# Moving a recurrence's copies to ScalarE, its output to a PSUM bank of its own, weight low parts to VectorE, and masks to fills

## The chip, the core and the metric

One core of one Trainium2 chip runs the whole program once. The metric is device time in microseconds (us) of one execution. The engines of the core are TensorE (PE in the profile; its weight loads are PEld), VectorE (DVE), ScalarE (ACT), GpSimd (POOL) and SyncE (SP). Each works through its own queue of instructions in order and waits on semaphores of the others.

## The reference

The program is a stack of layers on 512 tokens of width 1024: two layers of a first block (neighbourhood attention, differential attention, convolution), and then a second block of two layers, each with a feed-forward part, a mixer and another feed-forward part. Only the two mixers of the second block are touched here. The first mixer is a delta-rule recurrence over tokens, beside a gated linear recurrence:

```python
def rwkv7_step(S, inp):
    r_t, w_t, k_t, v_t, kk_t, a_t = inp
    sa = jnp.einsum("bhvk,bhk->bhv", S, -kk_t)
    S = (S * w_t[:, :, None, :]
         + jnp.einsum("bhv,bhk->bhvk", sa, kk_t * a_t)
         + jnp.einsum("bhv,bhk->bhvk", v_t, k_t))
    y = jnp.einsum("bhvk,bhk->bhv", S, r_t)
    return S, y
```

The second mixer is a stick-breaking attention, whose mask is strict (a token does not see itself):

```python
mask = k_pos[None, :] < q_pos[:, None]
log_1m = jnp.where(mask, jax.nn.log_sigmoid(-z), 0.0)
between = lax.cumsum(log_1m, axis=3, reverse=True) - log_1m
att = jnp.where(mask, jnp.exp(jax.nn.log_sigmoid(z) + between), 0.0)
```

## The kernel before

Everything is kept on the core. Large products are made in a split form: a weight chunk of 128x1024 is loaded by SyncE's DMA queue, ScalarE rounds it to its high part `whi` (line 366), another engine subtracts to get the low part `wlo` (line 368), and TensorE multiplies hi by hi, lo by hi and hi by lo (line 574). Which engine makes the low part is decided by name in `wchunk`: GpSimd for the chunks of the two mixers (`ein`, `eo`, `sq`, `sk`, `sv`), apart from five listed in `BEGIN`, and VectorE for all others. Of the 22 chunks of the first mixer's input projection (`ein`), 19 have their low part made by GpSimd.

**First mixer (`even`).** Eight heads are handled as four pairs, and the 512 tokens as eight chunks of 64. For each pair, `prep`, `inverse` and `tokens` work out the chunk matrices (mostly small VectorE operations), and `recur` then walks the eight chunks in order. The next pair's preparation and the projections' products are woven between the steps of `recur`, and a priority scheduler fixes the order of each engine when the program is built. A chunk of `recur` takes one PSUM bank `pc` (the profile calls it `mm`; the tag has two buffers) and goes: two products of the state `VS` with `G` (line 1747), a copy of the first to `Xs` by VectorE (1749) and of the second to `ya` by ScalarE (1750), a product with `Y` (1753), two copies of its halves into `VS`, one by ScalarE and one by VectorE (1755), a product with `B` that gives the next state (1759) and one with `MTr` that gives the rest of the output (1761), then the next state as the product plus the decayed state `SD` by VectorE (1767), `SD` for the chunk after by GpSimd (1771), and `ya` plus the second part by VectorE (1772). All five products of a chunk lie in columns of the one bank.

**Second mixer (`stick`).** For each of eight head pairs and four query blocks (32 units, of 512, 384, 256 and 128 keys), TensorE makes the scores (1406), ScalarE makes two sigmoids, `o` and `b` (1410, 1411), GpSimd masks the last 128 columns: `o` by a multiplication and an addition, `b` by a multiplication (1413 to 1415), with two 128x128 tables in `bc`; VectorE then runs a reversed running product over `o` for each of the two heads (1421), multiplies it into `b` (1422), and TensorE transposes `b` (1431) and multiplies by the values (1449). The projections of the next pair (line 574) run between.

Of the kernel before, what the change touches and what calls it, by code (L numbers as in the profile page):

```python
# [11 lines left out]
F32 = mybir.dt.float32  # L12
# [74 lines left out]
BEGIN = [('ein', 12), ('ein', 13), ('ein', 8), ('sv', 0), ('sk', 0)]  # L87
# [200 lines left out]
class Kern:  # L288
# [63 lines left out]
    def wchunk(self, name, i, n, split=True, extra=False, slot=None):  # L352
# [14 lines left out]
        eng = nc.gpsimd if name in ('ein', 'eo', 'sq', 'sk', 'sv') and (name, i) not in BEGIN else nc.vector  # L367
# [986 lines left out]
    def stick(self, sp, oh, ol, out):  # L1354
# [5 lines left out]
        bc = sp.tile([128, 2, 128], F32, name="bc")  # L1360
        nc.gpsimd.dma_start(bc, a['before'].rearrange("p (j n) -> p j n", j=2))
        before, notbefore = [bc[:, j].unsqueeze(1).to_broadcast([128, 2, 128]) for j in range(2)]
# [30 lines left out]
        class Unit:  # L1393
# [5 lines left out]
            def S(s):  # L1399
# [11 lines left out]
                nc.scalar.activation(b[:, :, :n], z[:, :, :n], AF.Sigmoid, scale=0.125)  # L1411
                d = slice(n - 128, n)
                nc.gpsimd.tensor_tensor(o[:, :, d], o[:, :, d], before, ALU.mult)  # L1413
                nc.gpsimd.tensor_tensor(o[:, :, d], o[:, :, d], notbefore, ALU.add)  # L1414
                nc.gpsimd.tensor_tensor(b[:, :, d], b[:, :, d], before, ALU.mult)
# [68 lines left out]
    def even(self, sp, oh, ol, room, out):  # L1484
# [251 lines left out]
        def recur(pr):  # L1736
# [5 lines left out]
            for c in range(8):  # L1742
                pc = self.mm()
                for j, cs in ((0, slice(0, 64)), (1, slice(192, 256))):
                    for h in range(2):
                        kr = slice(0, 128) if c else H[1 - h]
                        nc.tensor.matmul(pc[H[h], cs], G[h][kr, c, j], VS[kr, h, c], start=True, stop=True)
                Xs = sp.tile([128, 64], F32, name="Xs", tag="Xs", bufs=2)
                nc.vector.tensor_copy(Xs, pc[:, 0:64])
                nc.scalar.copy(ya[:, c], pc[:, 192:256])  # L1750
# [3 lines left out]
                for h in range(2):  # L1754
                    (nc.vector.tensor_copy if h else nc.scalar.copy)(VS[H[h], h, c], pc[H[h], 64:128])
# [4 lines left out]
                for h in range(2):  # L1760
                    nc.tensor.matmul(pc[H[h], 256:320], MTr[H[h], c], VS[H[h], h, c], start=True, stop=True)
                if c < 7:
                    for h in range(2):
                        if SD is None:
                            (nc.vector.tensor_copy if h else nc.scalar.copy)(VS[H[h], h, c + 1], pc[H[h], 128:192])
                        else:
                            nc.vector.tensor_tensor(VS[H[h], h, c + 1], pc[H[h], 128:192], SD[H[h]], ALU.add)
                if c < 6:
                    SD = sp.tile([128, 64], F32, name="SD", tag="SD", bufs=2)
                    for h in range(2):  # L1770
                        nc.gpsimd.tensor_scalar(SD[H[h]], VS[H[h], h, c + 1], dc[H[h], c + 1:c + 2], None, ALU.mult)
# [314 lines left out]
```

## Time and profile before

| | us |
|---|---|
| median of three runs | 3127.25 (3127.15 to 3130.33) |
| the profiled execution, its own time | 3127.6 |
| its span in the trace | 3125.4 |
| first mixer, from its first projections to the end of its recurrence | 1337 to 1690 |
| of that, the 32 chunks of the recurrence | 1403 to 1677 |
| second mixer, its 32 units | 2475 to 2725 |

The sum in the prediction is made against the profiled execution's 3127.6 us, which is 0.35 us above the median; the span and 2.2 us around it make it up. Positions such as 1403 are microseconds from the span's start. In the rows further down, the idle time of an engine is followed by what ended it ("<-ACT ya L1750" is ScalarE's write of `ya` on line 1750), and a granted clock of 1.00 is 2.4 GHz, one of 0.50 is 1.2 GHz.

### The profile page before, as it was taken

Reading aid. Unit: us, or ns where it says so; the run is one execution under the profiler, and the core shown is the slowest. Engines: PE = TensorE matmul, PEld = TensorE weight load, DVE = VectorE, ACT = ScalarE, POOL = GpSimd, SP = SyncE. Lnnn points to the kernel's source line nnn. Section 1 sums busy time; section 2 is a strip of 40 time slices with the busy share of each in tenths; the row PEclk is TensorE's granted clock in tenths of the full one; section 3 lists DMA queues with packets and bytes.
Section 4 is the critical chain, followed back from the end, with each engine's and each line's share of the span. In section 5 each row is a group of like instructions: output and inputs, shape, how many; then the busy total and the mean of one; then the engine's idle time right before and its main releaser. Section 6 shows DMA issues by size and latency. Waiting matters only on the chain. (4 is left out here: it accounts for less than half of the span.)

```text
span 3125.4 us, 47823 instructions
## 1 busy us (share of the span) xinstructions
PE 2968.1 (95%) x18806; PEld 2544.0 (81%) x18806; DVE 2198.8 (70%) x3818; ACT 1434.9 (46%) x2501; POOL 481.2 (15%) x597
## 2 busy tenths in 40 slices
PE   7999999999999999988898999989999988889998
PEld 4987887798878989865556899979898766779897
DVE  5968674767767949568774976859495566779494
ACT  5358654437644535342323544435353444445352
POOL 3010010111001000143334100010000455310000
PEclk9999999999999999999879999999999999999999
DMA  5232123231232423421003332433334211223233
GB/s 201 95 123 77 40 70 110 72 108 62 63 111 92 125 85 99 152 81 41 21 21 115 97 123 85 141 116 96 94 109 146 66 48 48 77 86 119 88 93 127
DMA packets 81681, 290.69 MB, mean 93 GB/s; under 512 B 9264, under 2 KB 9616, under 8 KB 81328
## 3 DMA queue, kind: packets, MB, share of 16 engines
q1 hardware_dynamic: 68688, 241.35, 24.4%
q10 hardware_dynamic: 7200, 26.22, 2.3%
q0 software_dynamic: 5568, 20.07, 2.0%
q8 instruction: 148, 2.42, 0.3%
q14 instruction: 77, 0.63, 0.1%
HBM read 272.92 MB, written 14.68 MB: 92 GB/s over the span
## 5 line engine op out<-in xcount | busy, mean ns | idle before, releaser
L366 ACT CAST whi<-wraw 128x1024 fp32r<-128x1024 f32 (+2 forms) x300 | 298.3, 1002 | 459.3 <-PE gm L574 120.2
L368 DVE TENSOR_TENSOR wlo<-wraw,whi 128x1024 fp32r<-128x1024 f32 (+2 forms) x254 | 300.2, 1189 | 271.4 <-ACT whi L366 265.0
L605 PE MATMUL acc<-whi,ah 128*128 128x512 f32 x704 | 225.2, 394 | 0.0
L605 PE MATMUL acc<-wlo,ah 128*128 128x512 f32 x704 | 225.0, 394 | 0.0
L605 PE MATMUL acc<-whi,al 128*128 128x512 f32 x704 | 224.7, 393 | 0.0
L574 PE MATMUL gm<-hh,whi 128*128 128x512 f32 (+1 forms) x752 | 210.0, 398 | 3.1 <-DVE ol L416 1.9
L400 ACT CAST whi<-wraw 128x512 fp32r<-128x512 f32 (+1 forms) x152 | 126.9, 837 | 168.3 <-PE acc L701 94.2
L574 PE MATMUL gm<-hl,whi 128*128 128x512 f32 (+1 forms) x752 | 195.6, 393 | 1.1 <-DVE hl L551 1.1
L574 PE MATMUL gm<-hh,wlo 128*128 128x512 f32 (+1 forms) x752 | 193.4, 391 | 0.0
L449 POOL DMA_DIRECT2D gb<-rows x13 | 7.5, 579 | 1193.2 <-DMA x<-xd 563.1
L605 PEld LDWEIGHTS acc<-whi,al 128*128 128x128 f32 x704 | 132.2, 188 | 30.7
L574 PEld LDWEIGHTS gm<-hl,whi 128*128 128x128 f32 x752 | 134.4, 197 | 27.4 <-DVE hl L551 1.8
L605 PEld LDWEIGHTS acc<-wlo,ah 128*128 128x128 f32 x704 | 131.9, 188 | 30.0
L574 PEld LDWEIGHTS gm<-hh,wlo 128*128 128x128 f32 x752 | 132.6, 194 | 28.8 <-issue 3.7
L401 DVE TENSOR_TENSOR wlo<-wraw,whi 128x512 fp32r<-128x512 f32 (+1 forms) x152 | 144.9, 955 | 15.9 <-ACT whi L400 15.8
L605 PEld LDWEIGHTS acc<-whi,ah 128*128 128x128 f32 x704 | 131.6, 188 | 29.6
L574 PEld LDWEIGHTS gm<-hh,whi 128*128 128x128 f32 x752 | 131.4, 195 | 29.3 <-PE gm L1384 2.9
L401 DVE TENSOR_TENSOR wlo<-s,whi 128x1024 fp32r<-128x1024 f32 x76 | 93.0, 1223 | 62.0 <-ACT whi L400 58.6
L368 POOL TENSOR_TENSOR wlo<-wraw,whi 128x1024 fp32r<-128x1024 f32 x46 | 118.2, 2571 | 88.9 <-PE gm L574 31.7
L400 ACT CAST whi<-uraw 128x1024 fp32r<-128x1024 f32 x76 | 79.9, 1051 | 94.5 <-issue 51.8
L1421 DVE TENSOR_TENSOR_SCAN o<-o,zero 128x512 f32<-128x512 f32 (+3 forms) x64 | 84.7, 1360 | 31.7 <-POOL o L1414 31.6
L701 PE MATMUL acc<-hh,wlo 128*128 128x256 f32 x608 | 96.5, 281 | 0.0
(586 smaller groups left out, 7614.9 us busy)
## 6 DMA issues: line engine op xcount, KB each, us to landing
wraw<-l_ffn SPq DMA_DIRECT2D x180, 512.0 KB, 3.7
uraw<-l_ffn SPq DMA_DIRECT2D x76, 512.0 KB, 3.6
wraw<-w_mod SPq DMA_DIRECT2D x48, 512.0 KB, 3.6
x<-xd ACTq DMA_DIRECT2D x24, 512.0 KB, 6.8
wraw<-ein SPq DMA_DIRECT2D x22, 512.0 KB, 3.6
xd<-x ACTq DMA_DIRECT2D x20, 512.0 KB, 2.6
wraw<-w_out SPq DMA_DIRECT2D x16, 512.0 KB, 3.6
gb<-rows POOLq DMA_DIRECT2D x13, 512.0 KB, 8.2
```

The costliest lines, as they stand in the source:

```text
L366: nc.scalar.copy(h[:, :n], r[:, :n])
L368: eng.tensor_tensor(l[:, :n], r[:, :n], h[:, :n].bitcast(F32), ALU.subtract)
L400: nc.scalar.copy(h, src)
L401: nc.vector.tensor_tensor(l, src, h.bitcast(F32), ALU.subtract)
L449: (q or self.nc.gpsimd).dma_start(g, self.a['rows'][ROWS.index(name):ROWS.index(name) + 1, :].broadcast_to([128, D]))
L574: self.nc.tensor.matmul(p, ww[:, k, :], hx[:, k, sl] if tiles is None else part(hx[:, k]), start=(n == 0), stop=(n == 3 * KC - 1))
L605: nc.tensor.matmul(accs[s], ax[:, k, t * 128:(t + 1) * 128], ws[ci][wi][:, (k - c0) * 512:(k - c0 + 1) * 512], start=(ci == 0 and pi == 0 ...
L701: self.nc.tensor.matmul(p, ws[wi][:, k], x[xi][:, k], start=n == 0, stop=n == 11)
L1421: nc.vector.tensor_tensor_scan(ro, ro, zero.to_broadcast([128, n]), 1.0, ALU.mult, ALU.add)
```

## The change

In the first mixer each chunk of the recurrence takes two banks instead of one: the output products go to `py`, where the second is accumulated onto the first by TensorE, so the early copy to `ya` and the late addition become one ScalarE copy at the chunk's end. `Xs`, both halves of `VS` and `SD` are made by ScalarE (the first state, which has no `SD`, is copied by VectorE in both halves). The low parts of all `ein` chunks are made by VectorE. In the second mixer the three masking operations and their table become two `affine_select` on GpSimd, which write a constant where the position is masked.

```diff
-BEGIN = [('ein', 12), ('ein', 13), ('ein', 8), ('sv', 0), ('sk', 0)]
+BEGIN = [('sv', 0), ('sk', 0)]
...
-        eng = nc.gpsimd if name in ('ein', 'eo', 'sq', 'sk', 'sv') and (name, i) not in BEGIN else nc.vector
+        eng = nc.gpsimd if name in ('eo', 'sq', 'sk', 'sv') and (name, i) not in BEGIN else nc.vector
...
-        bc = sp.tile([128, 2, 128], F32, name="bc")
-        nc.gpsimd.dma_start(bc, a['before'].rearrange("p (j n) -> p j n", j=2))
-        before, notbefore = [bc[:, j].unsqueeze(1).to_broadcast([128, 2, 128]) for j in range(2)]
+        one, nought = nc.gpsimd.to_reg(1.0), nc.gpsimd.to_reg(0.0)
...
-                nc.gpsimd.tensor_tensor(o[:, :, d], o[:, :, d], before, ALU.mult)
-                nc.gpsimd.tensor_tensor(o[:, :, d], o[:, :, d], notbefore, ALU.add)
-                nc.gpsimd.tensor_tensor(b[:, :, d], b[:, :, d], before, ALU.mult)
+                for u, fill in ((o, one), (b, nought)):
+                    nc.gpsimd.affine_select(u[:, :, d], u[:, :, d], pattern=[[0, 2], [-1, 128]], base=0, channel_multiplier=1,
+                                            compare_op=ALU.is_gt, fill=fill)
...
-                pc = self.mm()
-                for j, cs in ((0, slice(0, 64)), (1, slice(192, 256))):
+                pc, py = self.mm(), self.mm()
+                for j, p in ((0, pc), (1, py)):
                     for h in range(2):
                         kr = slice(0, 128) if c else H[1 - h]
-                        nc.tensor.matmul(pc[H[h], cs], G[h][kr, c, j], VS[kr, h, c], start=True, stop=True)
+                        nc.tensor.matmul(p[H[h], 0:64], G[h][kr, c, j], VS[kr, h, c], start=True, stop=j == 0)
...
-                nc.vector.tensor_copy(Xs, pc[:, 0:64])
-                nc.scalar.copy(ya[:, c], pc[:, 192:256])
+                nc.scalar.copy(Xs, pc[:, 0:64])
...
-                    (nc.vector.tensor_copy if h else nc.scalar.copy)(VS[H[h], h, c], pc[H[h], 64:128])
+                    nc.scalar.copy(VS[H[h], h, c], pc[H[h], 64:128])
...
-                    nc.tensor.matmul(pc[H[h], 256:320], MTr[H[h], c], VS[H[h], h, c], start=True, stop=True)
+                    nc.tensor.matmul(py[H[h], 0:64], MTr[H[h], c], VS[H[h], h, c], start=False, stop=True)
...
-                            (nc.vector.tensor_copy if h else nc.scalar.copy)(VS[H[h], h, c + 1], pc[H[h], 128:192])
+                            nc.vector.tensor_copy(VS[H[h], h, c + 1], pc[H[h], 128:192])
...
-                        nc.gpsimd.tensor_scalar(SD[H[h]], VS[H[h], h, c + 1], dc[H[h], c + 1:c + 2], None, ALU.mult)
-                nc.vector.tensor_tensor(ya[:, c], ya[:, c], pc[:, 256:320], ALU.add)
+                        nc.scalar.activation(SD[H[h]], VS[H[h], h, c + 1], AF.Copy, scale=dc[H[h], c + 1:c + 2])
+                nc.scalar.copy(ya[:, c], py[:, 0:64])
```

The line numbers of the changed kernel are one lower in this part. On VectorE, in the first pair's recurrence, before (`w`, `G`, `MTa` belong to the next pair's preparation):

```order
L1755 COPY VS<-mm 64x64
L1602 SCALAR_TENSOR_TENSOR w<-k,vecs,acc 128x512
L1767 TENSOR_TENSOR VS<-mm,SD 64x64
L1608 SCALAR_TENSOR_TENSOR G<-w,Dx 64x8x64
L1612 SCALAR_TENSOR_TENSOR w<-w 128x512
L1608 SCALAR_TENSOR_TENSOR G<-w,Dx 64x8x64
L1613 SCALAR_TENSOR_TENSOR w<-w 128x512
L1615 TENSOR_SCALAR w<-w,hv 128x512
L1767 TENSOR_TENSOR VS<-mm,SD 64x64
L1616 SCALAR_TENSOR_TENSOR w<-w,k 128x512
L1772 TENSOR_TENSOR ya<-ya,mm 128x64
L1619 TENSOR_TENSOR w<-w 128x512
```

and at the same place now:

```order
L1601 SCALAR_TENSOR_TENSOR w<-k,vecs,acc 128x512
L1766 TENSOR_TENSOR VS<-mm,SD 64x64
L1607 SCALAR_TENSOR_TENSOR G<-w,Dx 64x8x64
L1611 SCALAR_TENSOR_TENSOR w<-w 128x512
L1607 SCALAR_TENSOR_TENSOR G<-w,Dx 64x8x64
L1612 SCALAR_TENSOR_TENSOR w<-w 128x512
L1614 TENSOR_SCALAR w<-w,hv 128x512
L1766 TENSOR_TENSOR VS<-mm,SD 64x64
L1615 SCALAR_TENSOR_TENSOR w<-w,k 128x512
L368 TENSOR_TENSOR wlo<-wraw,whi 128x1024
L1618 TENSOR_TENSOR w<-w 128x512
```

The copy into `VS` and the addition into `ya` have left the queue, and a low part of a projection chunk stands in it. On ScalarE, in the same recurrence, before (`shl` is a step of the projections):

```order
L366 CAST whi<-wraw 128x1024
L1750 COPY ya<-mm 128x64
L1755 COPY VS<-mm 64x64
L366 CAST whi<-wraw 128x1024
L1541 ACTIVATE shl<-gm,vecs 128x512
L366 CAST whi<-wraw 128x1024
L1750 COPY ya<-mm 128x64
```

and now:

```order
L366 CAST whi<-wraw 128x1024
L1770 ACTIVATE SD<-VS,dc 64x64 x2
L1749 COPY Xs<-mm 128x64
L1754 COPY VS<-mm 64x64 x2
L1770 ACTIVATE SD<-VS,dc 64x64 x2
L1771 COPY ya<-mm 128x64
L366 CAST whi<-wraw 128x1024
```

All steps of a chunk but the new state now stand in one row on ScalarE, between the casts. On GpSimd in the second mixer, one unit and the low part behind it, before:

```order
L1413 TENSOR_TENSOR o<-o,bc 128x2x128
L1415 TENSOR_TENSOR b<-b,bc 128x2x128
L1414 TENSOR_TENSOR o<-o,bc 128x2x128
L368 TENSOR_TENSOR wlo<-wraw,whi 128x1024
L1413 TENSOR_TENSOR o<-o,bc 128x2x128
```

and now:

```order
L1413 AFFINE_SELECT o<-o 128x2x128
L1413 AFFINE_SELECT b<-b 128x2x128
L368 TENSOR_TENSOR wlo<-wraw,whi 128x1024
L1413 AFFINE_SELECT o<-o 128x2x128
L1413 AFFINE_SELECT b<-b 128x2x128
```

One operation fewer stands ahead of VectorE's running product, and the orders of TensorE, VectorE and ScalarE in the second mixer are unchanged.

## Rows read from the trace of the kernel before

**Rows 1.** The page's first part: busy time, share and instructions of each engine.

```profile
PE 2968.1 (95%) x18806; PEld 2544.0 (81%) x18806; DVE 2198.8 (70%) x3818; ACT 1434.9 (46%) x2501; POOL 481.2 (15%) x597
```

**Rows 2.** Busy time in stretches: length, engines, granted clock, DMA share, GB/s.

```profile
1403.00:1677.00 274.00, 245.47 (x1896) 157.65 (x1893) 204.87 (x619) 85.33 (x169) 111.18 (x134) 0.88 0.11 34
...
2475.00:2725.00 250.00, 221.50 (x1192) 174.05 (x1191) 174.03 (x202) 115.23 (x194) 132.95 (x113) 0.95 0.18 53
```

**Rows 3.** Waits of TensorE, 1403 to 1677: us in total, times, longest.

```profile
PE mm L1747 <- DVE VS L1767: 5.7, 5, 2.6
PE mm L1759 <- DVE VS L1755: 4.9, 5, 2.8
...
PE mm L1753 <- ACT ya L1750: 2.6, 4, 0.9
```

**Rows 4.** Waits of VectorE, the same stretch.

```profile
DVE VS L1755 <- ACT VS L1755: 11.1, 10, 3.4
...
DVE Xs L1749 <- PE mm L1747: 6.8, 10, 1.3
```

**Rows 5.** Waits of ScalarE, the same stretch.

```profile
ACT ya L1750 <- DVE Xs L1749: 51.4, 21, 6.2
ACT whi L366 <- PE gm L574: 42.8, 10, 9.6
```

**Rows 6.** Groups by form on VectorE, 1337 to 1690: busy, mean ns, idle before.

```profile
L1755 DVE COPY VS<-mm 64x64 f32<-64x64 f32 x32 | 7.2, 227 | 11.9 <-ACT VS L1755 11.1
...
L1772 DVE TENSOR_TENSOR ya<-ya,mm 128x64 f32<-128x64 f32 x32 | 7.0, 220 | 1.8 <-PE mm L1761 1.0
L1749 DVE COPY Xs<-mm 128x64 f32<-128x64 f32 x32 | 6.9, 219 | 7.0 <-PE mm L1747 6.8
```

**Rows 7.** Groups by form on ScalarE, 1337 to 1690.

```profile
L1755 ACT COPY VS<-mm 64x64 f32<-64x64 f32 x32 | 6.5, 205 | 32.8 <-PE mm L1753 29.8 <-PE acc L1633 3.0
```

**Rows 8.** Groups by form on GpSimd, 1337 to 1690.

```profile
L368 POOL TENSOR_TENSOR wlo<-wraw,whi 128x1024 fp32r<-128x1024 f32 x23 | 57.6, 2504 | 58.8 <-issue 27.6 <-PE gm L574 25.6 <-ACT whi L366 3.9
L1771 POOL TENSOR_SCALAR SD<-VS,dc 64x64 f32<-64x64 f32 x48 | 25.9, 540 | 45.9 <-DVE VS L1767 31.6 <-DVE Z L1706 7.3 <-ACT VS L1765 4.2
```

**Rows 9.** The page's costliest groups: low parts made by VectorE, whole program.

```profile
L368 DVE TENSOR_TENSOR wlo<-wraw,whi 128x1024 fp32r<-128x1024 f32 (+2 forms) x254 | 300.2, 1189 | 271.4 <-ACT whi L366 265.0
```

**Rows 10.** Timeline of VectorE, first mixer: start, us, instruction.

```profile
1421.19 0.16 DVE L436 SCALAR_TENSOR_TENSOR rs_tw<-rs_tw,rs_vw 128x8 f32<-128x8 f32 x1
...
1422.35 2.34 DVE L436 SCALAR_TENSOR_TENSOR rs_tw<-rs_tw,rs_vw 128x8 f32<-128x8 f32 x1
```

**Rows 11.** Timeline of GpSimd, the same place.

```profile
1422.31 2.35 POOL L368 TENSOR_TENSOR wlo<-wraw,whi 128x1024 fp32r<-128x1024 f32 x1
```

**Rows 12.** The chain that ended last, 2525 to 2600: start, us, what.

```profile
2524.40 0.74 POOL o L1413
...
2525.22 0.74 POOL o L1414
...
2525.98 3.94 DVE o L1421 x2
...
2544.25 1.74 POOL o L1413
...
2546.07 0.74 POOL o L1414
...
2546.84 4.45 DVE o L1421 x2
...
2551.93 5.50 PE gm L1449 x24
```

**Rows 13.** Waits of TensorE, 2440 to 2725.

```profile
PE gm L1449 <- DVE ql L416: 14.1, 5, 2.9
```

**Rows 14.** Groups by form on GpSimd, whole program: operations on 256 columns.

```profile
L550 POOL TENSOR_SCALAR hT<-hT,mod 128x256 f32<-128x256 f32 x8 | 9.3, 1164 | 13.7 <-ACT ch L549 13.7
...
L1084 POOL MEMSET lC<- 64x256 f32 x14 | 4.3, 305 | 72.3 <-PE acc L1091 43.7 <-issue 28.2
```

## Prediction

> **What bounds the kernel now.** I read the page's first part, then a table of stretches, then the waits inside the two stretches that the change touches. TensorE is busy 95% of the span [rows 1], so only the stretches where it is not can give anything. In the recurrence of the first mixer, 274 us long, it is busy 245.5 us: 28.5 us idle, at a mean granted clock of 0.88 [rows 2]. A mean of 0.88 is 12% of 274, or 33 us of full clock that was not granted, time spent at 1.2 GHz. The second mixer's units take 250 us, with TensorE busy 221.5, again 28.5 us idle, at 0.95 (12.5 us) [rows 2]. So the first mixer can give at most 28.5 + 33 = 61 us, the second at most 41.
>
> What holds TensorE in the recurrence are small hand-overs: 5.7 us for VectorE's new state, 4.9 for its copy into `VS`, 2.6 for ScalarE's `ya` [rows 3], 13.2 in all; the other 15.3 are spread over the next pair's preparation, nearly all VectorE's. VectorE is in turn busy 204.9 of 274 us [rows 2], and stands 11.1 us behind ScalarE's half of the same `VS` copy and 6.8 behind the product for `Xs` [rows 4]. ScalarE is busy 85 us of 274 [rows 2]. It waits 51.4 us for VectorE's `Xs`, since both read one bank [rows 5]: the reader will see that the two engines take turns on it, and that TensorE then waits for the second reader (the 2.6), though it needs only the first.
>
> In the second mixer the chain of waits runs, pair after pair, through the masks and the running product: 0.74 + 0.74 us of masking, then two products of together 3.94 us, and in the next 20 us once more 1.74 + 0.74 and 4.45 [rows 12]. TensorE waits 14.1 us, up to 2.9 at once, for `ql`, a VectorE step right behind that 4.45 us [rows 13].
>
> **The recurrence's copies.** VectorE loses 32 `Xs` of 219 ns, 32 `VS` of 227 and 32 additions of 220 [rows 6]: 7.0 + 7.3 + 7.0 = 21.3 us, less four first-state copies that come to it (4 x 0.23 = 0.9): 20.4. It also no longer waits the 11.1 + 6.8 us of [rows 4]. ScalarE gets 32 `Xs`, 32 - 4 `VS` and 48 `SD`, for which I take its own 205 ns [rows 7]: 108 x 0.205 = 22 us, hidden in its 189 idle us; without that cover they would lie on the chunk's path. `ya` stays one copy, only later. On TensorE's side the 2.6 us for `ya` go; of the 4.9 for `VS` I take 3, since two copies in a row on one engine need no hand-over between them; of the 5.7 for the new state 2, since VectorE's queue is shorter. Together 7.6 (at least nothing, if the same waits come back behind ScalarE, at most 13.2).
>
> **The second bank.** With `pc` and `py` a chunk holds both buffers of its tag. The next `pc` follows the new state anyway; the next `py` now waits for ScalarE's `ya`, with the product by `Y` and all of TensorE's queue behind it. At most one 0.21 us copy for each of 32 chunks, 6.7 us, if no longer operation stands ahead of it; I take 2, since products of the projections often stand between.
>
> **Low parts on VectorE, and less on GpSimd.** 19 operations come to VectorE; its own take 1189 ns [rows 9]: 22.6 us. Off GpSimd go 19 x 2.50 and 48 x 0.54 us [rows 8], 73 us. This also frees VectorE: a step of 0.16 us took 2.34 us [rows 10] while GpSimd made a low part over the same 2.35 us [rows 11]. So one removed low part frees VectorE of between nothing and 2.2 us, 19 of them between 0 and 42. Most VectorE steps have two inputs like the blocked one, but it is not always about to start one: I take 15. VectorE's balance is then 22.6 - 20.4 - 17.9 - 15 = -31 us. TensorE's 15.3 us of waits on the preparation should shrink with it; I take a third, 5.
>
> **The clock.** Less idle time should give some clock back. Nothing in the rows ties a fall to one wait, so the bounds are 0 and 33; I take a quarter, 8. First mixer: 7.6 - 2 + 5 + 8 = 18.6 us.
>
> **The masks.** Of the three operations per unit, two stood ahead of the running product, now one fill does. No row shows a fill. A GpSimd write of 256 columns without input takes 305 ns, a scalar operation with one input 1164 [rows 14], a two-input mask alone 740 [rows 12]. I take 0.74: a fill reads one input like the second and computes a position besides, but has no per-partition scalars. The 0.74 + 0.74 becomes 0.74. The 1.74 is a first mask that stood 1.0 us still, and I leave it that: 2.48 becomes 1.74. Per pair 1.5 us, and for seven of the eight pairs (the last has no projections beside it) 10.4; with the table's load gone, hidden before, and a little clock, 11. With 0.31 it would be 7 x 2 x (1.48 - 0.35) = 16, with 1.16 about 5. The long running product itself stays: the low parts of `sq`, `sk` and `sv` remain on GpSimd and will still fall between its two halves.
>
> By the Trainium skill (GPSIMD Engine Reference, section 4.1, Engine selection) GpSimd runs one-input elementwise work at about line rate and two-input work at half VectorE's; with the clock in its section 1 that would be a fill of 0.2 to 0.35 us (an estimate from that page), and the masks' gain the 16 just given. The 1164 ns row contradicts it by a factor of more than three, which is why I stay at 11.
>
> **Sum.** 3127.6 - 18.6 - 11 = 3098.0 us. The profiled execution lies 0.35 above the median, too little to shift it.
>
> **Rivals.**
> *Slower: low parts hold VectorE.* Made by VectorE, a low part stands in the same queue as the new state. Over the program VectorE waited 265 us for ScalarE's cast at 254 of them, 1.04 each [rows 9], and in the recurrence ten casts waited 42.8 us for TensorE, up to 9.6 [rows 5]. GpSimd took those waits at no cost. VectorE's balance of -31 is used up when a low part waits 31 / 19 = 1.6 us on the average; that point decides. If ten wait 4.3 us each, VectorE is 43 us worse, so 12 later than before; in the queue's order the recurrence waits with it, so I put 20 us on the path, against 5 left from the masks: 3143. Against it: the casts run two chunks ahead.
>
> *Fills are dear.* Above 1.48 us a fill lengthens the path. At 2.50, GpSimd's dearest row by the operation [rows 8], the second mixer pays 7 x 2 x 1.02 = +14, and with the first mixer's 18.6 the time is 3123: no change. No row on 256 columns is that long [rows 14]. The Trainium skill (GPSIMD Engine Reference, section 3.1) puts work that branches on its data at about 12 cycles per element, an estimate from that page of 2.6 us a fill; whether a fill branches no run here shows yet.
>
> *The bank takes it back.* If each `py` waits its full 0.21 and the small stalls keep the clock down, the 8 us do not come, and a clock of 0.82 instead of 0.88 costs 274 x 0.06 = 16 us more: -7.6 - 5 + 6.7 + 16 = +10, with the masks about 3127, no change. The Trainium skill (TensorE: Matmul & The Clock Gate, section A second HAM failure mode: psum-queue depth-cycling) tells of a kernel that cycles through PSUM banks and keeps losing its clock to short idles between groups. No row here shows that cause by itself.
>
> *Much better.* If VectorE's load was the whole limit, most of the 61 us comes: 45, and 16 from the masks: 3067.
>
> **Chances.** The forecast, 3082 to 3113: 0.45. Better than that: 0.13. Only one mixer gains much (3113 to 3121): 0.12. Dear fills, the bank, or gains and waits that cancel (within 0.2%, 6.3 us either way, about what a measurement of this kernel can tell from no change): 0.13. Slower: 0.17. So faster 0.70, same 0.13, slower 0.17. The range that leaves out 2 in 10 goes from 3066 to 3136; the likeliest case's own is 3082 to 3113.
>
> **What would show it.** In the profile after: the recurrence shorter than 274 us by about 19, with a granted clock above 0.88 and TensorE's wait for `ya` gone; GpSimd near 38 us in it and VectorE's 0.16 us steps no longer at 2 us; idle time ahead of VectorE's low parts in this stretch under 1.6 us each; fills near 0.74 us, running products starting one operation after their sigmoid, and the units' stretch some 11 us shorter than 250. The forecast is wrong if ScalarE's casts stand idle ahead of `Xs` while TensorE waits for it, if TensorE waits for `ya` from the chunk before, or if a fill takes over 1.5 us.

## The result and the profile after

The changed kernel takes 3080.89 us in the median of four runs (3075.25 to 3083.43), against 3127.2 (3125.67 to 3130.33) for the kernel before on the same chip: a ratio of 0.9848, 95% interval 0.9831 to 0.9865, by which 47 us are gained. The profiled execution took 3083.43 us, its span 3081.7.

First a table of stretches of the kernel before, by stage. A stage runs from TensorE's last product of the feed-forward part ahead of the mixer to its first of the next one; the row of 232.1 us is the second mixer's 32 units alone. Columns as in [rows 2].

```profile
1320.10:1767.70 447.60, 397.21 (x2787) 281.77 (x2786) 315.56 (x826) 158.94 (x282) 168.03 (x200) 0.90 0.19 62
...
2476.80:2708.90 232.10, 203.86 (x1093) 159.52 (x1092) 164.31 (x186) 108.56 (x181) 129.94 (x110) 0.94 0.18 53
...
2441.50:2806.70 365.20, 324.22 (x1802) 264.98 (x1801) 239.58 (x283) 163.28 (x274) 160.99 (x144) 0.94 0.21 65
```

The same view of the changed kernel, with the recurrence as its first row.

```profile
1398.00:1657.50 259.50, 242.36 (x1911) 155.13 (x1910) 178.94 (x546) 112.20 (x275) 58.43 (x83) 0.89 0.11 32
...
1324.70:1752.80 428.10, 392.99 (x2786) 279.06 (x2785) 293.86 (x754) 187.13 (x390) 97.04 (x133) 0.92 0.20 65
...
2461.30:2666.80 205.50, 192.53 (x1093) 152.52 (x1092) 150.49 (x187) 108.85 (x182) 83.98 (x79) 0.98 0.20 60
...
2426.00:2763.10 337.10, 311.41 (x1802) 257.24 (x1801) 224.25 (x283) 163.14 (x274) 112.31 (x111) 0.97 0.22 70
```

The reader subtracts TensorE's busy time from the length. The first mixer's stage is 19.5 us shorter: its idle time went from 50.4 to 35.1, its busy time fell by 4.2. The second mixer's is 28.1 us shorter: idle 41.0 to 25.7, and 12.8 us less busy time for the same 1802 products, at a granted clock of 0.97 in place of 0.94. Outside the two stages, where the code is unchanged, this execution took 3.9 us more. In the first mixer the three stretches of before (ahead of the recurrence, in it, behind it) took 83.3, 272.3 and 92.0 us, those of now 73.3, 259.5 and 95.3.

TensorE's waits in the first mixer's stage of the changed kernel; they answer to [rows 3].

```profile
PE mm L1760 <- ACT VS L1754: 3.1, 6, 1.2
PE mm L1747 <- DVE Z L1705: 1.9, 1, 1.9
...
PE acc L1720 <- DVE X L1713: 1.0, 2, 0.8
...
PE mm L1747 <- DVE VS L1766: 0.5, 2, 0.3
...
PE mm L1752 <- ACT Xs L1749: 0.5, 2, 0.3
```

The waits on the state's hand-overs, 14.9 us before over all their rows, are 5.3, of which 0.3 for `ya` of the chunk before. Those on the next pair's preparation (rows of 0.6 us and more), 15.7 before, are 5.0. Part of this comes back elsewhere: for other steps of ScalarE, whose queue is now longer (`B`, `u`, `gb`, `xb`), TensorE waits 4.4 us in place of 0.7. Two groups of ScalarE and VectorE, the first in the recurrence, the second in the whole stage; they answer to [rows 8, 9].

```profile
L1770 ACT ACTIVATE SD<-VS,dc 64x64 f32<-64x64 f32 x48 | 16.5, 345 | 25.0 <-DVE VS L1766 24.2
```

```profile
L368 DVE TENSOR_TENSOR wlo<-wraw,whi 128x1024 fp32r<-128x1024 f32 x26 | 33.8, 1301 | 10.4 <-ACT whi L366 4.7 <-PE gm L574 2.2 <-issue 2.1
```

VectorE stands idle 0.4 us ahead of a low part, a quarter of the 1.6 at which it would have cost. In the second mixer's units, the masks as fills:

```profile
L1413 POOL TENSOR_SCALAR_AFFINE_SELECT b<-b 128x256 f32<-128x256 f32 x31 | 25.0, 807 | 9.7 <-ACT b L1409 9.4
L1413 POOL TENSOR_SCALAR_AFFINE_SELECT o<-o 128x256 f32<-128x256 f32 x31 | 13.4, 431 | 94.5 <-ACT o L1408 94.5
```

and TensorE's waits in the same stretch, which answer to [rows 13] and to one row of the kernel before beside it:

```profile
PE gm L1448 <- DVE ql L416: 8.2, 5, 1.7
PE mm L1430 <- DVE w3l L416: 2.9, 1, 2.9
```

```profile
PE mm L1431 <- DVE w3l L416: 9.2, 6, 3.9
```

`ql` is the low part of the next pair's queries, `w3l` that of transposed `b`; VectorE reads both out of PSUM, and TensorE's products with the values (L1448) and its transposes (L1430) wait for them. The wait for `ql` fell by 5.9 us, that for `w3l` by 6.3, and others by 3.0: with the idle time of the units, 28.2 and 13.0, this comes out.

A fill of `o` took 0.43 us on the average, not 0.74. Now VectorE at the place of [rows 12], the kernel before:

```profile
2544.18 1.21 DVE L1422 TENSOR_TENSOR b<-b,o 128x1022 f32<-128x1022 f32 x1
2546.84 4.45 DVE L1421 TENSOR_TENSOR_SCAN o<-o,zero 128x384 f32<-128x384 f32 x2 [1.44 <-POOL o L1414]
2551.21 0.66 DVE L416 TENSOR_TENSOR ql<-gm,qh 128x512 fp32r<-128x512 f32 x1
2551.80 0.41 DVE L416 TENSOR_TENSOR w1l<-mm,w1h 128x256 fp32r<-128x256 f32 x1
2552.13 0.94 DVE L1422 TENSOR_TENSOR b<-b,o 128x766 f32<-128x766 f32 x1
```

and the changed kernel, VectorE and then GpSimd:

```profile
2521.24 1.97 DVE L1420 TENSOR_TENSOR_SCAN o<-o,zero 128x384 f32<-128x384 f32 x2 [0.77 <-POOL o L1413]
2523.31 2.91 DVE L1421 TENSOR_TENSOR b<-b,o 128x766 f32<-128x766 f32 x1
2526.14 0.41 DVE L416 TENSOR_TENSOR w1l<-mm,w1h 128x256 fp32r<-128x256 f32 x1
2526.48 0.67 DVE L416 TENSOR_TENSOR ql<-gm,qh 128x512 fp32r<-128x512 f32 x1
```

```profile
2520.80 0.41 POOL L1413 TENSOR_SCALAR_AFFINE_SELECT o<-o 128x256 f32<-128x256 f32 x1 [3.86 <-ACT o L1408]
2521.50 0.90 POOL L1413 TENSOR_SCALAR_AFFINE_SELECT b<-b 128x256 f32<-128x256 f32 x1 [0.29 <-ACT b L1409]
2522.37 3.04 POOL L368 TENSOR_TENSOR wlo<-wraw,whi 128x1024 fp32r<-128x1024 f32 x1
```

Two things are to be seen. The running product is no longer split by the low part (1.97 us for 4.45); the low part now lies on the multiplication into `b`, 2.91 us for 0.94. And the order has changed: `ql` stood ahead of that multiplication and now stands behind it. **So the sentence ahead of the prediction, that the orders of TensorE, VectorE and ScalarE in the second mixer are unchanged, is wrong:** only TensorE's is. The scheduler, which sees cheaper masks, places them otherwise: in the traces of that stage 24 of VectorE's 283 instructions stand at another place, and one of ScalarE's 274. VectorE's order there before (the running product is called SCALAR_TENSOR_TENSOR in it):

```
L1421 SCALAR_TENSOR_TENSOR o<-o,zero 128x384 x2
L416 TENSOR_TENSOR ql<-gm,qh 128x512
L416 TENSOR_TENSOR w1l<-mm,w1h 128x2x128
L1422 TENSOR_TENSOR b<-b,o 128x2x383
```

and now:

```
L1420 SCALAR_TENSOR_TENSOR o<-o,zero 128x384 x2
L1421 TENSOR_TENSOR b<-b,o 128x2x383
L416 TENSOR_TENSOR w1l<-mm,w1h 128x2x128
L416 TENSOR_TENSOR ql<-gm,qh 128x512
```

The low part and the multiplication hold each other up: 2.91 us with the low part beside it, 0.94 without. The Trainium skill (SBUF — State Buffer, section SBUF: two separate sides) says that a VectorE operation with two inputs in SBUF and a GpSimd operation that reads SBUF exclude each other for a whole instruction. The rows agree: GpSimd's low part ends at 2525.41, and the multiplication 0.81 us later.

### The profile page after: what moved, and what is told of

Same layout as the page of the kernel before. It is cut to its first block, busy times and chain, and to the rows that moved or that the text cites. A ratio compares the mean times of both kernels' runs of the same rounds, so it can differ in the third digit from the quotient of the medians.

```text
span 3081.7 us, 47754 instructions
## 1 busy us (share of the span) xinstructions
PE 2953.0 (96%) x18806; PEld 2534.9 (82%) x18806; DVE 2161.2 (70%) x3745; ACT 1463.1 (47%) x2609; POOL 361.6 (12%) x497
## 5 line engine op out<-in xcount | busy, mean ns | idle before, releaser
L368 DVE TENSOR_TENSOR wlo<-wraw,whi 128x1024 fp32r<-128x1024 f32 (+2 forms) x273 | 322.6, 1189 | 284.1 <-ACT whi L366 272.1
L574 PEld LDWEIGHTS gm<-hh,wlo 128*128 128x128 f32 x752 | 130.7, 192 | 28.1 <-issue 3.2
L701 PE MATMUL acc<-hl,whi 128*128 128x256 f32 x608 | 96.5, 281 | 0.0
L701 PE MATMUL acc<-hh,whi 128*128 128x256 f32 x608 | 96.4, 281 | 0.0
```

Source lines behind the costliest of these rows:

```text
L368: eng.tensor_tensor(l[:, :n], r[:, :n], h[:, :n].bitcast(F32), ALU.subtract)
L574: self.nc.tensor.matmul(p, ww[:, k, :], hx[:, k, sl] if tiles is None else part(hx[:, k]), start=(n == 0), stop=(n == 3 * KC - 1))
L701: self.nc.tensor.matmul(p, ws[wi][:, k], x[xi][:, k], start=n == 0, stop=n == 11)
```

## The experiments

All of them in one table: the median of each, its ratio to the kernel before with the 95% interval, then from its profile the length of the two mixers' stages, the units' stretch with TensorE's idle time in it, and its granted clock there. The first mixer's stage in executions with the very same instructions there (the changed kernel, e5_twice, e6_late, e7_lowdve) lies between 423.7 and 428.3; the second's (the changed kernel, e1_fills, e8_sdpool, e9_bank, e10_onebank) between 337.1 and 341.0. Differences below 5 us in a stage say nothing.

| | median us | ratio | first | second | units (idle, clock) |
|---|---|---|---|---|---|
| before | 3127.2 | 1 | 447.6 | 365.2 | 232.1 (28.2, 0.94) |
| after | 3080.9 | 0.9848 (0.9831 to 0.9865) | 428.1 | 337.1 | 205.5 (13.0, 0.98) |
| e1_fills | 3102.4 | 0.9929 (0.9916 to 0.9942) | 447.8 | 341.0 | 208.2 (13.0, 0.97) |
| e2_low | 3109.9 | 0.9948 (0.9935 to 0.9961) | 432.3 | 362.9 | 229.4 (29.1, 0.96) |
| e3_recur | 3121.4 | 0.9990 (0.9981 to 0.9999) | 447.3 | 361.3 | 229.0 (26.6, 0.95) |
| e4_noadd | 3114.1 | 0.9967 (0.9954 to 0.9979) | 447.4 | 351.4 | 219.2 (19.8, 0.95) |
| e5_twice | 3078.9 | 0.9850 (0.9837 to 0.9863) | 428.3 | 335.5 | 202.2 (10.2, 0.99) |
| e6_late | 3085.9 | 0.9873 (0.9860 to 0.9886) | 426.9 | 344.7 | 212.4 (15.0, 0.96) |
| e7_lowdve | 3066.8 | 0.9813 (0.9799 to 0.9826) | 423.7 | 327.1 | 196.9 (5.1, 0.98) |
| e8_sdpool | 3081.5 | 0.9862 (0.9848 to 0.9875) | 426.7 | 339.4 | 206.6 (13.0, 0.98) |
| e9_bank | 3076.3 | 0.9850 (0.9837 to 0.9864) | 426.9 | 339.4 | 206.5 (13.0, 0.98) |
| e10_onebank | 3072.6 | 0.9834 (0.9821 to 0.9848) | 417.0 | 341.0 | 208.2 (13.0, 0.97) |
| e11_alldve | 3065.3 | 0.9812 (0.9799 to 0.9825) | 423.6 | 326.6 | 195.6 (5.1, 0.99) |
| e12_lowonly | 3094.7 | 0.9905 (0.9891 to 0.9919) | 431.7 | 350.6 | 217.7 (23.2, 0.98) |

Microseconds gained below are the ratio's distance from 1 times 3125.

**The three parts alone.** e1_fills takes the masks' lines of the change alone, e2_low the low parts', e3_recur the recurrence's.

```diff
-                nc.gpsimd.tensor_tensor(o[:, :, d], o[:, :, d], before, ALU.mult)
...
+                    nc.gpsimd.affine_select(u[:, :, d], u[:, :, d], pattern=[[0, 2], [-1, 128]], base=0, channel_multiplier=1,
```

> Kernel before with the two fills alone. Account from the two traces: the second mixer is shorter by 28 us and nothing else moves, 3127 - 28 = 3099. Forecast's terms: a mask of 0.74 less per unit, 11 us, 3116. Rival (the second mixer's gain needs the first mixer's edits, by a position or a state of the clock carried over): about 3116 as well, and the missing 17 us show up in no run of one part alone. Fill seen at 0.41 us where VectorE's product does not overlap it.

```diff
-BEGIN = [('ein', 12), ('ein', 13), ('ein', 8), ('sv', 0), ('sk', 0)]
+BEGIN = [('sv', 0), ('sk', 0)]
...
-        eng = nc.gpsimd if name in ('ein', 'eo', 'sq', 'sk', 'sv') and (name, i) not in BEGIN else nc.vector
+        eng = nc.gpsimd if name in ('eo', 'sq', 'sk', 'sv') and (name, i) not in BEGIN else nc.vector
```

> Kernel before with the low parts of the first input projection on VectorE alone. Account from the traces: 10 us in the pairs' preparation ahead of the recurrence, a few more in the recurrence since a freed port gives back more than a low part costs: 3127 - 12 = 3115. Forecast's balance: VectorE gains 22.6 us of work and gets at most 15 back while SD stays on GpSimd; a third of the 8 to 13 us on the path, 3127 to 3132. Slower rival (low parts wait for their casts in front of the new state): 3135 and more.

```diff
-                pc = self.mm()
+                pc, py = self.mm(), self.mm()
...
-                        nc.gpsimd.tensor_scalar(SD[H[h]], VS[H[h], h, c + 1], dc[H[h], c + 1:c + 2], None, ALU.mult)
-                nc.vector.tensor_tensor(ya[:, c], ya[:, c], pc[:, 256:320], ALU.add)
+                        nc.scalar.activation(SD[H[h]], VS[H[h], h, c + 1], AF.Copy, scale=dc[H[h], c + 1:c + 2])
+                nc.scalar.copy(ya[:, c], py[:, 0:64])
```

> Kernel before with the recurrence's edits alone (own bank, one late copy, Xs, VS and SD on ScalarE). Account from the traces: what the low parts do not explain of the first mixer's 19.5 us, about 8, in the 32 chunks: 3119. Forecast's terms: copies 7.6 less 2 for the bank, plus a part of 5 and 8 for preparation and clock, 12: 3115. Rival (the bank and ScalarE's longer row take it back): 3127, with TensorE waiting for ya from the chunk before or for SD's state.

Measured: 22, 16 and 3 us, 41.6 in all against 47 for the whole, a difference that the intervals (3 to 5 us either way each) do not tell from nothing. e1_fills came 3 us short of its account's 3099 and far from the rival's 3116, so the fills' gain needs nothing from the first mixer; e2_low gained more than its account's 12 us, and the forecast's balance and the slower rival fell; e3_recur lies between its account's 3119 and the rival's 3127. Low parts alone, e2_low, TensorE's stretches ahead of the recurrence, in it, and the stage:

```profile
1322.00:1395.30 73.30, 70.30 (x418) 55.49 (x416) 55.03 (x140) 36.93 (x53) 13.07 (x26) 1.00 0.31 102
1395.30:1661.10 265.80, 234.52 (x1918) 156.04 (x1917) 200.32 (x638) 84.75 (x169) 87.94 (x132) 0.89 0.12 36
...
1322.00:1754.30 432.30, 383.77 (x2787) 278.79 (x2786) 313.55 (x846) 158.42 (x282) 122.78 (x181) 0.92 0.20 64
```

Its stage is 15.3 us shorter, but only 1.9 of that is idle time (50.4 to 48.5); 13.4 are busy time, at a clock of 0.92 for 0.90 (ahead of the recurrence 1.00, with 73.3 us for 83.3; 39 of TensorE's 457 instructions there now stand behind it). Waits on the preparation fell from 15.7 to 7.4 us, 5.6 of it ahead of the recurrence, but those on the hand-overs rose from 14.9 to 17.9. For the recurrence alone, e3_recur, the waits of TensorE in the stage:

```profile
PE acc L1721 <- DVE X L1714: 5.6, 4, 2.6
PE acc L1595 <- DVE rs_ow L437: 4.9, 2, 3.5
PE acc L1653 <- DVE G L1649: 3.4, 3, 2.3
PE mm L1761 <- ACT VS L1755: 2.9, 3, 1.4
```

The hand-overs fell from 14.9 to about 7 us as intended, but TensorE then met the preparation sooner: 15.7 became 18.8 (the first three rows are the main ones). So the recurrence's edits, bank and copies together, are worth little while GpSimd makes the low parts of `ein`.

**Where the masks' 22 us come from.** First, from the kernel before, the forecast's own case (e4_noadd): one two-input operation ahead of the running product. The kernel leaves the addition out.

```diff
-                nc.gpsimd.tensor_tensor(o[:, :, d], o[:, :, d], notbefore, ALU.add)
```

> Kernel before with the addition left out of the mask of o, so that masked positions hold 0 where they should hold 1 (a part of the computation is left out): one two-input operation ahead of the running product, as the forecast assumed of a fill at 0.74 us. Forecast: 11 us, 3116. Account that lays most of the 28 us to one operation fewer and to stalls short enough for the clock to stay up: 18 to 24 us, 3103 to 3109. Account that lays it to the fill's own form (one input, 0.41 us, not held up by VectorE): only 5 to 8 us, 3119 to 3122.

Measured: 10 us, near the forecast's number (11). TensorE's, VectorE's and ScalarE's orders are those of the changed kernel there. So one operation fewer, with the order that follows, is worth 10, and fills in place of the other two 12 more.

From the changed kernel then, one fill more: in e5_twice ahead of the product, in e6_late behind its start.

```diff
-                for u, fill in ((o, one), (b, nought)):
+                for u, fill in ((o, one), (o, one), (b, nought)):
```

> Changed kernel (3081) with the fill of o made twice (the second writes the same values), so that 0.86 us of GpSimd stand ahead of the running product, as much as the one two-input mask took in the run with the addition left out (0.857 on the average), but in the form of fills. If the time ahead of the product is what counts, the second mixer goes back to what that run showed: +10 to +12 us, 3091 to 3093, with the 384-column products split by a low part again. If the fill's form counts (one input, not held up by VectorE), only 7 pairs x 2 x 0.43 = 6 us or less come, 3087.

```diff
-                for u, fill in ((o, one), (b, nought)):
+                for u, fill in ((o, one), (b, nought), (b, nought)):
```

> Changed kernel with the fill of b made twice: the same load on GpSimd as in the run with o filled twice, but behind the point at which the running product may start; it delays only the low parts of the projections behind it. If the time ahead of the product is what counts: no change, 3080 to 3083. If GpSimd's load or the place at which its low part falls on VectorE's work counts: several us either way (3075 or 3088), with another of VectorE's operations at 2 us in place of the multiplication of 766 columns.

Both expectations for e5_twice fell: with a second fill ahead of the product nothing was lost (3078.9). The reason stands in the order: with the dearer masks the scheduler gave back exactly the orders of before, `ql` ahead of the multiplication. Its VectorE at the same place, and TensorE's waits:

```profile
2521.71 4.16 DVE L1420 TENSOR_TENSOR_SCAN o<-o,zero 128x384 f32<-128x384 f32 x2 [0.78 <-POOL o L1413]
2525.79 0.66 DVE L416 TENSOR_TENSOR ql<-gm,qh 128x512 fp32r<-128x512 f32 x1
```

```profile
PE gm L1448 <- DVE ql L416: 4.9, 5, 1.2
PE mm L1430 <- DVE w3l L416: 3.3, 2, 2.9
```

The running product is split again (4.16 us), and TensorE nevertheless waits less for `ql` than in the changed kernel. In e6_late, where nothing more stands ahead of the product, the units take 212.4 us against 205.5: the second fill of `b` delays the low part, and the multiplication ahead of `ql` behind it (VectorE's order at this place is the changed kernel's). So it is not the time ahead of the product alone. TensorE's wait for `ql` follows, in all runs, the time from the first operation on `o` of the 384-column unit to the start of `ql`, read from the timelines (the pair in the middle), beside that wait:

| | mask to `ql`, us | wait for `ql` in five pairs, us |
|---|---|---|
| before | 6.96 | 14.1 |
| e4_noadd | 6.57 | 12.8 |
| e12_lowonly | 6.28 | 10.3 |
| e6_late | 6.05 | 10.0 |
| after | 5.68 | 8.2 |
| e5_twice | 5.06 | 4.9 |
| e7_lowdve | 3.78 | 0 |

From before to after the distance shrank by 1.28 us and the wait by 5.9 / 5 = 1.18 for a pair; to e5_twice by 1.90 and 1.84. A microsecond on this path is a microsecond of TensorE's wait for `ql`, whichever operation it is in. That is a part of the units' gain only: of the 26.6 us from before to after, 5.9 are this wait, 9.4 other idle time (6.3 of it for `w3l`), and 11.3 busy time at a granted clock of 0.98 for 0.94. Less idle time and a higher clock mostly go together, but not always: e12_lowonly below has 23.2 us idle at 0.98, e4_noadd 19.8 at 0.95. What raised the clock is not shown. In e6_late, too, 4.9 of the units' 6.9 us are busy time, at 0.96.

**GpSimd's low parts in the second mixer.** e7_lowdve moves, in the changed kernel, those of `sq`, `sk` and `sv` to VectorE too.

```diff
-        eng = nc.gpsimd if name in ('eo', 'sq', 'sk', 'sv') and (name, i) not in BEGIN else nc.vector
+        eng = nc.gpsimd if name == 'eo' else nc.vector
```

> Changed kernel with the low parts of sq, sk and sv on VectorE as well (22 more there), so that GpSimd holds only fills in the second mixer. If what is left of TensorE's 13 us of waits there comes from VectorE being held up by a low part (27 us over what its operations take undisturbed): the multiplications of 766 and 510 columns fall from 2.4 and 2.0 us to about 1.0, and the time to 3072 to 3078. Rival: 17 low parts of 1.19 us in VectorE's queue delay the running products and ql by more than that, TensorE's waits for ql rise above 8.2 us, and the time is 3085 to 3092.

e11_alldve moves those of `eo` as well.

```diff
-        eng = nc.gpsimd if name == 'eo' else nc.vector
+        eng = nc.vector
```

> Changed kernel with every low part on VectorE, those of eo too, on top of the run with sq, sk and sv there (3066.8). If a low part on GpSimd costs by what it holds up on VectorE: the 7 to 10 low parts of eo overlap the tail of the first mixer, where VectorE runs 6.7 us over its undisturbed durations; a part of that comes, 3062 to 3066. Rival (VectorE's queue in the tail is what TensorE waits for, 6.4 us at y): 3068 to 3072.

e12_lowonly has the line of e7_lowdve in the kernel before, with masks and recurrence untouched.

```diff
-        eng = nc.gpsimd if name in ('ein', 'eo', 'sq', 'sk', 'sv') and (name, i) not in BEGIN else nc.vector
+        eng = nc.gpsimd if name == 'eo' else nc.vector
```

> Kernel before with all low parts of ein, sq, sk and sv on VectorE, the three masks and the recurrence untouched. If the collision of low parts with VectorE is what the second mixer mostly lost, and the fills only moved it from the running product to the multiplication: 16 us as with ein alone and 20 or more in the second mixer, 3088 to 3092. If the masks' own operations are the loss (held up by VectorE, and its products held up by them): only 5 to 10 us more than with ein alone, 3100 to 3105, with the first mask still at 0.97 us and TensorE still waiting for ql over 10 us.

Measured: e7_lowdve is 11 us faster than the changed kernel by the ratios, more than its own account gave. In its units, VectorE's low parts and the multiplication that was held up, then TensorE's waits:

```profile
L368 DVE TENSOR_TENSOR wlo<-wraw,whi 128x1024 fp32r<-128x1024 f32 x20 | 24.1, 1204 | 4.4 <-PE gm L574 4.4
...
L1421 DVE TENSOR_TENSOR b<-b,o 128x766 f32<-128x766 f32 x8 | 7.6, 944 | 0.2
```

```profile
PE mm L1430 <- DVE w3l L416: 2.9, 1, 2.9
PE gm L574 <- DVE ol L416: 1.9, 5, 0.4
```

The wait for `ql` is gone. The units are 8.6 us shorter, with VectorE less busy (148.2 against 150.5) although it makes 17 low parts more. e11_alldve is the same within the measurement; it is the fastest version run, with e7_lowdve, and both beat both kernels. e12_lowonly fell between its two expectations: 30 us, 13 more than e2_low. So neither explains away the other: in the second mixer's stage the fills are worth 24 us with the low parts on GpSimd (365.2 to 341.0, e1_fills), and 23.5 with those of `sq`, `sk` and `sv` on VectorE (350.6 to 327.1, e12_lowonly to e7_lowdve). The mutual hold-up of low parts and VectorE is thus one loss, and the masks' own time on the path another.

**SD, the copies and the bank.** All from the changed kernel. First SD alone back on GpSimd, e8_sdpool.

```diff
-                        nc.scalar.activation(SD[H[h]], VS[H[h], h, c + 1], AF.Copy, scale=dc[H[h], c + 1:c + 2])
+                        nc.gpsimd.tensor_scalar(SD[H[h]], VS[H[h], h, c + 1], dc[H[h], c + 1:c + 2], None, ALU.mult)
```

> Changed kernel with the decayed state SD on GpSimd again. ScalarE's SD takes 0.344 us, not the 0.205 of the forecast, but ScalarE is idle half of the recurrence, and SD is needed a chunk later: account from the traces, no change, 3079 to 3083 (within 2 us). If SD on ScalarE is what takes the recurrence's gain back (the run of the recurrence's edits alone was 3 us faster, no more): 3076. If SD on GpSimd holds up VectorE's queue, which waits for it at the new state: 3084 to 3087.

e9_bank has the same line, and besides

```diff
-                nc.scalar.copy(Xs, pc[:, 0:64])
+                nc.vector.tensor_copy(Xs, pc[:, 0:64])
...
-                    nc.scalar.copy(VS[H[h], h, c], pc[H[h], 64:128])
+                    (nc.vector.tensor_copy if h else nc.scalar.copy)(VS[H[h], h, c], pc[H[h], 64:128])
```

> Changed kernel with the own bank and its late ya copy kept, but Xs and half of the VS copies on VectorE and SD on GpSimd as before. Account from the runs of single parts (the low parts give nearly all of the first mixer's gain): 3084 to 3087, since the recurrence's part is worth 3 to 4 us, and TensorE's wait for ya (6.8 us when the low parts alone were moved) stays gone while that for VS comes back. Forecast's terms: the copies are worth 7.6 and a part of the preparation's 5 and the clock's 8: 3090 or more. If the bank is the whole of it: 3081.

e10_onebank puts all products of a chunk into one bank again, with `ya` copied early:

```diff
-                pc, py = self.mm(), self.mm()
+                pc = self.mm()
...
+                nc.scalar.copy(ya[:, c], pc[:, 192:256])
...
-                nc.scalar.copy(ya[:, c], py[:, 0:64])
+                nc.vector.tensor_tensor(ya[:, c], ya[:, c], pc[:, 256:320], ALU.add)
```

> Changed kernel with one bank again: both outputs in columns of pc, ya copied early by ScalarE and completed by VectorE's addition, but Xs, VS and SD on ScalarE. Account from the traces (ScalarE's copies remove the hand-overs, the bank is neither cost nor gain): 3081 to 3084, with ScalarE's ya copy right behind Xs and no turn-taking. If the bank carries the gain (readers of pc wait on each other): 3085 to 3090 with TensorE waiting for ya at the product with Y. If the second bank costs (the forecast put 2 us on it, its rival 6.7): 3075 to 3079.

Where SD is made does not matter (3081.5). e9_bank came out at the changed kernel's time, against its account: on top of the bank the copies on ScalarE give nothing that can be told, though TensorE's hand-over waits are 12.0 us in e9_bank's stage and 5.3 in the changed kernel's. But e10_onebank, the copies without the bank, is the shortest first mixer of all: 417.0 us, 6.6 below the shortest of the others with the low parts moved; of its expectations the one in which the second bank costs is the nearest. The times' intervals of e10_onebank and the changed kernel overlap, so this rests on the stage.

With the low parts of `ein` on VectorE there are runs of all four cases. One bank and the copies as before: 432.3 and 431.7 us (e2_low, e12_lowonly). The copies and SD moved, one bank: 417.0. The second bank, the copies as before: 426.9 (e9_bank). Both: 423.7 to 428.3. So the copies alone give 15 us, the bank alone 5, hardly outside the spread, and with the copies on ScalarE the bank takes 7 to 11 back. By the ratios the copies and SD alone are worth 13 us in time (e10_onebank against e2_low and e1_fills together), with some 7 us of uncertainty. What TensorE does there, the output products with `MTr` in the recurrence of the changed kernel, of e9_bank, and of e10_onebank:

```profile
L1760 PE MATMUL mm<-VS,MTr 64*64 64x64 f32 x128 | 17.8, 260 | 3.2 <-ACT VS L1754 3.1
```

```profile
L1760 PE MATMUL mm<-VS,MTr 64*64 64x64 f32 x128 | 21.1, 261 | 1.6 <-ACT VS L1754 1.6
```

```profile
L1761 PE MATMUL mm<-VS,MTr 64*64 64x64 f32 x128 | 12.0, 257 | 0.5 <-ACT VS L1755 0.5
```

The same 128 products of the same 0.26 us each keep TensorE busy 17.8, 21.1 and 12.0 us (12.6 before). The timelines show why: in the changed kernel one head's products often stand apart from the other's,

```profile
1501.55 0.33 PE L1760 MATMUL mm<-VS,MTr 64*64 64x64 f32 x2
1501.81 0.34 PE L1758 MATMUL mm<-VS,B 128*64 128x64 f32 x4
1502.07 0.33 PE L1760 MATMUL mm<-VS,MTr 64*64 64x64 f32 x2
1502.33 0.50 PE L574 MATMUL gm<-hl,whi 128*128 128x512 f32 x1
```

while in the kernel before, and in e10_onebank (second fence), both heads run side by side in the same 0.33 us:

```profile
1514.36 0.34 PE L1759 MATMUL mm<-VS,B 128*64 128x64 f32 x4
1514.62 0.33 PE L1761 MATMUL mm<-VS,MTr 64*64 64x64 f32 x4
1514.88 0.50 PE L574 MATMUL gm<-hh,wlo 128*128 128x512 f32 x1
```

```profile
1497.86 0.33 PE L1761 MATMUL mm<-VS,MTr 64*64 64x64 f32 x4
```

In TensorE's order the two heads stand together in 29 of 32 chunks before, 30 in e10_onebank, 15 after and 4 in e9_bank. In every run with `py` the scheduler places the two apart more often; whether that comes from the tile of its own or from the accumulation into it was not separated. 14 chunks more apart make the line's busy time 5.2 us longer. From start to start the products with `B` and `MTr` take 0.78 us apart and 0.52 together, which for 14 chunks is an estimate of 3.6 us. That is a part of the 7 to 11 us that the bank takes back; the rest stays open.

## Why the prediction was right in direction, and where its size was off

The median of 3080.9 us lies 1 us below the range that was forecast, 3082 to 3113, in the case "better than that". The direction and the places were right; the masks' term was half of what came.

**The masks, 11 us forecast, 22 measured: the mis-sized term.** The step "I take 0.74" set a fill at the price of a two-input mask; it took 0.43, so the 16 us given for a short fill were nearer. The row of 1164 ns that spoke against a short fill was misread: it is a mean of operations that VectorE held up in part. The view of that line (count, shortest/median/longest):

```profile
L550 POOL TENSOR_SCALAR hT<-hT,mod x12: 569/1093/2202, 38.1 to 58.8; 128x256 f32<-128x256 f32 x8, 128x512 f32<-128x512 f32 x4
```

The shortest two, 0.57 and 0.59 us on 256 columns, ran while VectorE did a one-input operation; the longest, 2.20 on as many columns, beside low parts that VectorE made. The kernel with one two-input mask (0.86 us on the average) gave 10 us, so the sum was about right for its assumption. The step that left the 1.74 as it was failed as well: the first mask stood behind the multiplication of the unit before, and the earlier, shorter masks no longer meet it there. "A little clock" was too little: of the units' 26.6 us, 15.3 are idle time and 11.3 busy time at 0.98 for 0.94. The prediction looked at the wait for `ql` alone; the 9.2 us for `w3l`, of which 6.3 went, it left out. And "the long running product itself stays" was wrong: it fell from 4.45 to 1.97 us, and the low part moved to the multiplication behind it. Since the order changed with it, `ql` pays that: with the old order, two fills ahead of the product (e5_twice) do as well as one with the new.

**The copies, 7.6.** Measured on the hand-overs: 9.6 us of TensorE's waits. Right in place, and near in size, in the whole change. What they are worth in time depends on the other edits, which the prediction did not see: with the low parts on GpSimd, bank and copies together give 3 us, since the preparation's waits take their place; with the low parts moved and one bank the copies shorten the stage by 15.

**The second bank, 2.** The wait for `ya` that it was put on did not come. It cost something else: 7 to 11 us of the stage with the copies on ScalarE, of which 3.6 to 5.2 are heads set apart in TensorE's queue. The price of 6.7 in its bound was nearer, by another mechanism and so by luck. With the copies on VectorE the bank cost nothing (426.9 against 432).

**Low parts on VectorE.** They are the larger part of the first mixer's gain (15 of the 19.5 in the stages), more than the 5 us on the preparation and a share of the clock credited to them; 10 us of it lie ahead of the recurrence, a stretch that the prediction did not look at. Nine of the 19 low parts that GpSimd made start there, so GpSimd's busy time in the recurrence is 58.4 us and not near the 38 that the prediction named as a sign. The other sign came: no step of VectorE like the one that took 2.34 us takes more than 0.17 in the recurrence. The preparation's waits fell by 10.7 in the whole change, twice the third that was taken. SD cost ScalarE 0.345 us each, not 0.205, and as argued it is hidden.

**The clock, 8.** The first mixer's busy time fell 4.2, or about 8 to 9 without what the separated heads cost. The recurrence itself rose only from 0.88 to 0.89, against the forecast of more; that stretch's 12.8 us came mostly from idle time (28.5 to 17.1). The bound of 33 us is right as a loss, but not as time spent at 1.2 GHz: with two levels a mean of 0.88 means 66 of the 274 us there. The first mixer's sum, 18.6 against 19.5 in the profiles, came out right partly because these errors cancel, which is luck.

**The rivals.** Low parts holding VectorE: refuted, 0.4 us ahead of each, and e2_low gains. Dear fills: refuted, 0.43 us. The estimate of 0.2 to 0.35 us from the Trainium skill (GPSIMD Engine Reference, section 4.1, Engine selection) was nearer than the 1164 ns row that spoke against it; the 2.6 us estimated from the branching figure of the same page of the Trainium skill (section 3.1) are not what this fill took. The bank taking it all back: refuted, though with the copies on ScalarE it does cost. The outcome lies between the forecast's 3098 and the "much better" case's 3067.

**What stays open.** In e2_low the recurrence's busy time fell 9.3 us while the clock there rose only from 0.88 to 0.89 and idle time did not fall; the projections' products took 412, 393 and 387 in place of 418, 417 and 407 ns on the average in their three groups over the stage, and what made them so was not separated. Nor is it shown what raised the clock in the second mixer's units, 11.3 us. One bank together with all low parts on VectorE was not run.

## What to carry to other kernels

Where a scheduler sets the order, a cheaper operation changes the order of other engines too: compare the order of every engine around the waiting instruction, and price the whole path up to it, here from the first mask to `ql`. When GpSimd and VectorE both read SBUF, moving a long GpSimd operation to VectorE can cost less than it frees: here 1.2 us on VectorE against 1.5 to 2 us of holding it up, at the very operations that TensorE waits for. A hand-over that is shortened pays only if the next thing that TensorE needs is ready: the recurrence's edits gave 3 us alone, and the copies among them 15 us of the stage once the low parts were moved and the bank left single. Edits that are put together in one change are worth trying in all their pairs.

## What the runs showed of the hardware that was not expected

A fill of 128x256 on GpSimd takes 0.41 us undisturbed, less than the 0.74 of a two-input operation on the same columns, but VectorE holds it up too: beside the running product the fill of `b` took 0.90 to 0.96. ScalarE needs 0.345 us for a 64x64 copy with a scale per partition, and 0.206 for a plain copy of 64x64 out of PSUM. Two 64x64 products of different halves run side by side in 0.33 us if they are neighbours in TensorE's queue; set apart, the second starts a slot of its own, 0.26 us more.
